# Two output weights placed above the normed rows, the rows in pieces, and key chunks of 272, 256 and 512 columns

## The chip, the cores and the metric

The kernel runs on one core of one Trainium2 chip. The metric is the device time of one execution in microseconds (us), the median of the runs shown. The core's engines work side by side, each through a queue of its own in a fixed order: TensorE (PE in the profile; PEld is its loading of weights), VectorE (DVE), ScalarE (ACT), GpSimd (POOL), and SyncE (SP), which here only issues transfers. Matmuls write to PSUM banks of 128 x 512 float32; everything else that is worked on lies in SBUF.

## The reference

One layer of a hybrid encoder over 1024 rows of width 1024, with 16 learned rows in front (1040 in all):

```
u     = rms_norm(h, norm_mix_w)
proj  = u @ w_in                       # fq fk fv ff hq hf hi hg
fox   = attention(fq, fk, fv, log_sigmoid(ff + bias))   # 8 heads x 64, causal,
                                       # score + sum of log f between key and query
hgrn  = rms_norm(recurrence(hq, hf, hi)) * silu(hg)     # 4 heads, 128 x 128 state
h     = h + concat(fox, hgrn) @ w_out
u     = rms_norm(h, norm_ffn_w)
h     = h + (silu(u @ w_gate) * (u @ w_up)) @ w_down    # 2816 wide
out   = rms_norm(h, norm_final_w)[16:]
```

All inputs and outputs are float32.

## The kernel before, in words

Every product of float32 matrices is made of three matmuls: each operand is split into a rounded part (hi) and the rest (lo), and `mm3` (L171 to L173) adds hi·hi, hi·lo and lo·hi. The split of an operand is one cast on ACT and one subtraction on DVE (`split`, L139 and L140).

The stages, in the order in which they are written:

1. Rows are normed, transposed by PE and kept as `u`, two tiles (hi and lo) of 8 x 1136 columns each, in a pool of their own (`uT`). For odd row tiles a mirrored copy is made on POOL (L256).
2. The recurrence, head by head (`hgrn_proj`, `hgrn_compute`), and the values of the attention (`fox_v`).
3. The attention in four pairs of heads. `fox_proj` multiplies `u` by a pair's key and query weights (`form1`): the keys in the chunks of `FULL`, the queries in the two chunks of `REAL`. The first chunk of each is made at once; the rest (`rest()`: two key chunks, one of queries) is written after group 0 of the pair. Keys and queries of pairs 0 and 2 lie in the pool `fxk0`, those of 1 and 3 in `fxk1`. `fox_compute` runs four groups of 256 query rows, each for both heads: scores (L577, L578), the gate bias with a running minimum on DVE (L583), the exponential on ACT (L588), transposes (L596, L608), a split (L612, L613), and the product with the values (L618). Group g needs keys up to 16 + 256(g + 1).
4. The output projection. Its eight weight blocks (128 rows of `w_out` each) go through a staging tile `w_st` (two of them in the pool `w1`, used by every weight of the kernel), then a cast (L691) and two subtractions (L693) by `load_wo`. Blocks 4 to 7 belong to the recurrent heads, 0 to 3 to the attention. `out_half` multiplies the recurrent half of row tiles 0 and 1 and keeps the sums in `halves`; `out_proj` does the rest, tile by tile in `ORDER`, and adds the residual.
5. Norm, then the gated feed-forward in Strassen-like block products, whose sums and splits are made on DVE and ACT (`pair`, `ffn_sums`, `ffn_load`), the down projection, and the last norm.

SBUF is shared between pools that are opened and closed like stacks, one from the left and one from the right. A tile of a new pool waits for the last readers of the tiles that lay in its place. So the pools `op` (working tiles of the output stage) and `wo` (its weights), which take the place of `uT`, can be written only after `rest()` of the last pair has read `u` for the last time. They are opened by `after_group`, which `fox_compute` calls behind each group of the last pair:

```
def after_group(g):
    if g == 0:
        uT_pool.__exit__(None, None, None)
        op, wo = op_pool.__enter__(), wo_pool.__enter__()
        load_wo(WO1)          # blocks 4, 5, 6, 7
    if g == 1:
        out_half(ORDER[:2])
        load_wo(WO2)          # blocks 0, 1, 2, 3
```

The order on each engine, and that of the transfers on SP, is set when the program is built. What is written earlier goes first, unless by the planner's own estimate it isn't ready and something later is; so dense products written after a group are put between its steps, where their operands are planned to be there. On the chip the order stays, even where the times come out otherwise.

Of the kernel before, what the change touches and what calls it, by code (L numbers as in the profile page):

```python
# [25 lines left out]
UW = U0 + L  # L26
NT = SEQ // P
# [12 lines left out]
WO1 = (4, 5, 6, 7)  # L40
WO2 = (0, 1, 2, 3)
# [6 lines left out]
def f32(ap):  # L48
    return ap.bitcast(F32)
# [3 lines left out]
def hybrid_trunk(  # L53
# [64 lines left out]
    uT_pool = left("uT")  # L118
    uT = uT_pool.__enter__()
    u = (uT.tile([P, KT, UW], F32R, name="u_hi"), uT.tile([P, KT, UW], F32R, name="u_lo"))  # L120

# [20 lines left out]
    def norm_transpose(u, xt, rows, wb, xn_pool, col):  # L142
# [6 lines left out]
        for g in range(2):  # L149
            pt = bank("tr")  # L150
            p3 = pt.rearrange("p (k t) -> p k t", t=P)
            for k in range(4):
                pe.transpose(p3[:, k, :rows], xn[:rows, (4 * g + k) * P:(4 * g + k + 1) * P], ident[:rows, :rows])
            hi = u[0][:, 4 * g:4 * g + 4, col:col + rows]
            act.copy(hi, p3[:, :, :rows])
            vec.tensor_sub(u[1][:, 4 * g:4 * g + 4, col:col + rows], p3[:, :, :rows], f32(hi))
# [18 lines left out]
    def form1(u, w, c0, n):  # L175
        o = dense()
        hi, lo = w
        for k in range(KT):
            mm3(o[:, :n], hi[:, k, :], lo[:, k, :], u[0][:, k, U0 + c0:U0 + c0 + n], u[1][:, k, U0 + c0:U0 + c0 + n], k == 0, k == KT - 1)
        return o[:, :n]  # L180

    FULL = ((0, 272), (272, 384), (656, 384))
# [13 lines left out]
    def form2(w, col, c0, n, rows=P, v=u):  # L196
        o = dense()
        for k in range(KT):
            mm3(o[:rows, :n], v[0][:, k, col:col + rows], v[1][:, k, col:col + rows],
# [3 lines left out]
    def meta_stack(um):  # L203
        pool.memset(f32(um), 0.0)
        for r0, s_ in zip((0, 32), u):
# [13 lines left out]
    with ExitStack() as norm_ctx:  # L219
# [4 lines left out]
        def hi_tile(slot, rows, col):  # L224
# [3 lines left out]
            else:  # L228
                v, col = (flips.pop(slot), 0) if slot in flips else (u, col)
                act.copy(hvt, form2(whi, col, 0, 512, rows, v))  # L230
# [9 lines left out]
        for i, (slot, rows, col) in enumerate(TILES):  # L240
# [9 lines left out]
            norm_transpose(u, xt, rows, wb, npool, col)  # L250
# [101 lines left out]
    def hgrn_proj(h):  # L352
# [4 lines left out]
        for c0, n in FULL:  # L357
            o = form1(u, w, c0, n)
# [12 lines left out]
        for (c, sc, tag, lst) in ((C_HQ, float(P) ** -0.5, "hg_q", qs), (C_HG, 1.0, "hg_s", sgs)):  # L371
            w = load_m(c + h * P, w_in[0])
            for c0, n in REAL:
                o = form1(u, w, c0, n)
# [139 lines left out]
    def fox_proj(p, fxk):  # L514
# [7 lines left out]
        def keys(i):  # L522
            c0, n = FULL[i]
            o = form1(u, wk, c0, n)
# [4 lines left out]
        def queries(i):  # L529
            c0, n = REAL[i]  # L530
            o = form1(u, wq, c0, n)
# [151 lines left out]
    wos, op, wo = {}, None, None  # L683

    def load_wo(ks):
        for k in ks:
            st = w1.tile([P, D], F32, name="w_st", tag="w_st")
            sync.dma_start(out=st, in_=w_out[0, k * P:(k + 1) * P, :])
            hi = wo.tile([P, D], F32R, name=f"woh{k}")
            lo = wo.tile([P, D], F32R, name=f"wol{k}")  # L690
            act.copy(hi, st)  # L691
            for hs in (slice(0, 512), slice(512, 1024)):
                vec.tensor_sub(lo[:, hs], st[:, hs], f32(hi[:, hs]))  # L693
            wos[k] = (hi, lo)

    halves = {}
    op_pool, wo_pool = left("op", 2), left("wo")

    def out_half(ts):
        mt, mh, ml = (op.tile([P, KT, P], d, name=n_, tag=n_, bufs=1) for n_, d in (("mt", F32), ("mh", F32R), ("ml", F32R)))  # L700
# [4 lines left out]
        for i, t in enumerate(ts):  # L705
            halves[t] = op.tile([P, D], F32, name="h2", tag="h2")
            for hs in (slice(0, 512), slice(512, 1024)):
                o = dense()
                for k in range(4):
                    j = 4 * i + k  # L710
                    mm3(o, mh[:, j, :], ml[:, j, :], wos[4 + k][0][:, hs], wos[4 + k][1][:, hs], k == 0, k == 3)
                act.copy(halves[t][:, hs], o)

    def after_group(g):
        nonlocal op, wo
# [25 lines left out]
    wb2 = op.tile([P, D], F32, name="wb2", bufs=1)  # L741
    sync.dma_start(out=wb2, in_=norm_ffn_w[0, :].partition_broadcast(P))

    def out_proj(t):
        ts_ = slice(t * P, (t + 1) * P)
        mt = op.tile([P, KT, P], F32, name="mt", tag="mt", bufs=1)
        mh = op.tile([P, KT, P], F32R, name="mh", tag="mh", bufs=1)
        ml = op.tile([P, KT, P], F32R, name="ml", tag="ml", bufs=1)
# [4 lines left out]
        ht = op.tile([P, D], F32, name="ht", tag="ht")  # L753
# [19 lines left out]
    def norm2_first(t, ht=None, keep_psum=False):  # L773
        if ht is None:
            ht = op.tile([P, D], F32, name="h2", tag="h2")
            sync.dma_start(out=ht, in_=h_dram[t])
        s = op.tile([P, KT, P], F32, name="sT", tag="ml" if t == 7 else "sT", bufs=1)
# [7 lines left out]
        xn = op.tile([P, D], F32, name="xn", tag="h2")  # L785
# [39 lines left out]
    def ffn_raw(m):  # L825
        sts = []
        for wsrc in (w_ffn_gate, w_ffn_up):
            st = w1.tile([P, KT, P], F32, name="w_st", tag="w_st")
# [50 lines left out]
    for i, t in enumerate(ORDER):  # L879
        if i < NT - 1:  # L880
            hts[ORDER[i + 1]] = out_proj(ORDER[i + 1])
        else:
            wo_pool.__exit__(None, None, None)
# [5 lines left out]
        p_, tag = ((w1, "w_hi"), (w1, "w_lo"), (op, "mt"), (op, "mh"))[t - 4]  # L889
        tas[t - 4] = p_.tile([P, KT, P], F32, name=f"ta{t}", tag=tag, **({"bufs": 1} if p_ is op else {}))  # L890
        if t < 6:
            s_, pts_, = norm2_rest(norm2_first(t, hts[t], True))
# [8 lines left out]
    spare = [op.tile([P, KT, P], F32R, name=n_, tag=n_) for n_ in ("h2", "ht")]  # L901
    raw1 = ffn_raw(1)
# [19 lines left out]
    op_pool.__exit__(None, None, None)  # L922
# [281 lines left out]
```

## Time and profile before

| | us |
|---|---|
| runs | 1296.81, 1296.89, 1297.60 |
| median | 1296.89 |
| the profiled execution | 1297.19 |
| its span, first to last instruction | 1295.2 |
| PE busy | 1263.7 (98%) |
| DVE busy | 908.6 (70%) |
| ACT busy | 620.8 (48%) |

The profile is of one execution. Its lines name the line of the kernel, the engine, the operation, the tiles (written <- read) and the shape. In the lists of waits the columns are: the engine and tile that waited, what it waited for, us in total, times, longest. In the windows they are: the stretch and its length, then busy us and instructions of PE, PEld, DVE, ACT and POOL, the mean clock granted to TensorE (1.00 is full), the busy share of the transfer engines, and GB/s. A list of a single tile's instructions leaves out the engines that have none. In timelines: start, duration, engine, line, operation, and in brackets the idle time before it with what ended it. The last pair of heads lies at about 496 to 582 us, the output stage from there to about 651, and the feed-forward begins there.

### The profile page before, as it was taken

The numbers are of one execution on the slowest core, as the hardware profiler recorded it, in microseconds if no ns is written. First come the engines' busy times: TensorE is split into PE (matmuls) and PEld (weight loads), VectorE is DVE, ScalarE is ACT, GpSimd is POOL, SyncE is SP. The second block draws the span as 40 slices with busy tenths as digits, with TensorE's granted clock in tenths as the row PEclk, the third lists the DMA queues.
The fourth block names the chain that finished last, engine by engine and source line by source line (L and its number), as shares of the span: only waits on it lengthen the run. The fifth ranks groups of instructions, "written<-read, shape, count | busy, mean of one in ns | idle before, by whom it ended". The sixth has DMA issues, their size and how long they took to land.

```text
span 1295.2 us, 18497 instructions
## 1 busy us (share of the span) xinstructions
PE 1263.7 (98%) x6553; PEld 1066.5 (82%) x6553; DVE 908.6 (70%) x1889; ACT 620.8 (48%) x1334; POOL 126.4 (10%) x260
## 2 busy tenths in 40 slices
PE   8999999999899999899999999999999999999997
PEld 6888898988788888778868888888888888888886
DVE  6467666575597877796788766666666664697777
ACT  6356656464567666664453333233323333443364
POOL 1220101010334342210000000000000000000000
PEclk8999999999999999999999999999999999999999
DMA  7231212123222121533314323333332337854452
GB/s 255 74 115 45 73 42 74 58 60 115 66 92 63 59 63 47 180 111 116 127 49 139 123 82 121 122 111 106 118 122 74 114 122 265 305 194 147 122 170 82
DMA packets 135196, 146.37 MB, mean 113 GB/s; under 512 B 6984, under 2 KB 95368, under 8 KB 135104
## 3 DMA queue, kind: packets, MB, share of 16 engines
q1 hardware_dynamic: 135104, 145.19, 34.4%
q8 instruction: 52, 0.85, 0.3%
q14 instruction: 40, 0.33, 0.1%
HBM read 105.98 MB, written 39.19 MB: 112 GB/s over the span
## 4 chain that ended last, share of the span: by engine, by line
PE 81%; DVE 9%; ACT 4%; issue 2%; DMA 2%; POOL 1%; SPq 0%; DVEq 0%; ACTq 0%; POOLq 0%
PE pb L171 10%; PE pb L173 10%; PE pb L172 10%; PE dense L173 8%; PE dense L171 8%; PE dense L172 8%; PE g L171 4%; PE g L172 4%; PE g L173 4%; PE o L618 3%; PE tr L608 2%; PE g L577 1%; PE g L578 1%; DMA w_st<-in_w_in_dram 1%; PE o L172 1%
## 5 line engine op out<-in xcount | busy, mean ns | idle before, releaser
L172 PE MATMUL dense<-u_lo,w_hi 128*128 128x512 f32 (+2 forms) x384 | 141.0, 367 | 0.0
L171 PE MATMUL dense<-u_hi,w_hi 128*128 128x512 f32 (+2 forms) x384 | 140.2, 365 | 0.0
L173 PE MATMUL dense<-u_hi,w_lo 128*128 128x512 f32 (+2 forms) x384 | 139.5, 363 | 0.0
L172 PE MATMUL pb<-T_lo,bh 128*128 128x512 f32 x352 | 137.3, 390 | 0.3 <-DVE T_lo L140 0.2
L173 PE MATMUL pb<-T_hi,bl 128*128 128x512 f32 x352 | 136.9, 389 | 0.1
L171 PE MATMUL pb<-T_hi,bh 128*128 128x512 f32 x352 | 136.8, 390 | 0.2 <-ACT bh L139 0.2
L139 ACT CAST bh<-sS 128x512 fp32r<-128x512 f32 x88 | 54.3, 621 | 150.2 <-DVE sS L846 69.3
L139 ACT CAST h_hi<-h_st 128x1024 fp32r<-128x1024 f32 (+1 forms) x43 | 41.8, 972 | 82.3 <-PE o L172 37.8
L172 PEld LDWEIGHTS pb<-T_lo,bh 128*128 128x128 f32 x352 | 66.1, 188 | 15.0 <-DVE T_lo L140 1.2
L171 PEld LDWEIGHTS pb<-T_hi,bh 128*128 128x128 f32 x352 | 66.0, 188 | 14.4 <-ACT bh L139 0.6
L173 PEld LDWEIGHTS dense<-u_hi,w_lo 128*128 128x128 f32 x384 | 72.5, 189 | 6.2
L173 PEld LDWEIGHTS pb<-T_hi,bl 128*128 128x128 f32 x352 | 66.1, 188 | 14.0 <-DVE bl L140 0.4
L172 PEld LDWEIGHTS dense<-u_lo,w_hi 128*128 128x128 f32 x384 | 72.8, 190 | 5.8
L171 PEld LDWEIGHTS dense<-u_hi,w_hi 128*128 128x128 f32 x384 | 72.8, 190 | 5.7
L171 PE MATMUL pb<-w_hi,h_hi 128*128 128x512 f32 x198 | 77.0, 389 | 0.0
L172 PE MATMUL pb<-w_lo,h_hi 128*128 128x512 f32 x198 | 77.0, 389 | 0.0
L173 PE MATMUL pb<-w_hi,h_lo 128*128 128x512 f32 x198 | 77.0, 389 | 0.0
L140 DVE TENSOR_TENSOR w_lo<-w_st,w_hi 128x1024 fp32r<-128x1024 f32 (+1 forms) x41 | 49.8, 1214 | 36.8 <-ACT w_hi L139 36.6
L140 DVE TENSOR_TENSOR h_lo<-h_st,h_hi 128x1024 fp32r<-128x1024 f32 (+1 forms) x43 | 48.3, 1123 | 29.2 <-ACT h_hi L139 28.6
L139 ACT CAST w_hi<-w_st 128x1024 fp32r<-128x1024 f32 (+1 forms) x47 | 48.9, 1041 | 40.0 <-PE dense L172 17.3
L171 PE MATMUL g<-B_hi,w_hi 128*128 128x512 f32 x168 | 65.7, 391 | 0.8 <-ACT p L874 0.7
L172 PE MATMUL g<-B_lo,w_hi 128*128 128x512 f32 x168 | 65.4, 389 | 0.0
(861 smaller groups left out, 3344.1 us busy)
## 6 DMA issues: line engine op xcount, KB each, us to landing
w_st<-in_w_in_dram SPq DMA_DIRECT2D x24, 512.0 KB, 4.0
w_st<-in_w_ffn_gate_dram SPq DMA_DIRECT2D x22, 512.0 KB, 3.7
w_st<-in_w_ffn_up_dram SPq DMA_DIRECT2D x22, 512.0 KB, 3.9
B<-in_w_ffn_down_dram SPq DMA_DIRECT2D x20, 512.0 KB, 6.1
h_st<-S SPq DMA_DIRECT2D x20, 512.0 KB, 3.8
h_st<-A SPq DMA_DIRECT2D x15, 512.0 KB, 4.3
A<-g SPq DMA_DIRECT2D x22, 256.0 KB, 2.0
S<-u SPq DMA_DIRECT2D x22, 256.0 KB, 2.9
```

The source lines that it names most:

```text
L139: later(act.copy(hi, src))
L140: return later((engine or vec).tensor_sub(lo, src, f32(hi)))
L171: pe.matmul(o, lhsT=ah, rhs=bh, start=first, stop=False, skip_group_check=skip)
L172: pe.matmul(o, lhsT=ah, rhs=bl, start=False, stop=False, skip_group_check=skip)
L173: pe.matmul(o, lhsT=al, rhs=bh, start=False, stop=last, skip_group_check=skip)
L577: pe.matmul(sc[:, :w], lhsT=QA[:, P * i:P * (i + 1)], rhs=KS[:, c0:c0 + w], start=True, stop=False)
L578: pe.matmul(sc[:, :w], lhsT=QB[:, P * ii:P * (ii + 1)], rhs=KS[:, c0:c0 + w], start=False, stop=True)
L608: pe.transpose(pt[:, o + ii * P:o + (ii + 1) * P], Ss[ii][:, c:c + P], ident)
L618: m = pe.matmul(ob[:, q0:256], lhsT=vt[:, blk, :], rhs=r[:, q0:256], start=blk == NT, stop=blk == 2 * g + 1 and i == 3)
```

## The change

- **Rows in pieces.** The pool of `u` becomes two, `uh` and `ul`, and the tiles six: `ua_hi` and `ua_lo` hold the first 640 columns (all 8 blocks of the depth), `ub_hi0`, `ub_hi1` (four blocks each) and `ub_lo` the other 496. `u_k` and `u_half` find the place. The writes of `norm_transpose` and the mirrored copies go by halves of the depth, so an odd row tile has four mirrored copies of half the size for two.
- **Key chunks.** `FULL` goes from 272, 384, 384 to 272, 256, 512, so that a chunk ends where the first piece ends.
- **Early part.** A new pool `woe` is opened above the two pools of `u`, in the place of `fxk0`, before the last pair. Into it go, ahead of `fox_compute(3)`, the recurrent half of row tiles 0 and 1 with its split (`half_parts`, taken out of `out_half`), and weight blocks 4 and 5.
- **The output stage takes the pieces' places.** After group 0, five wide tiles are opened, each over one piece; `Slots` hands out rows of 1024 numbers of them under the old names. Blocks 6 and 7 and the hi of block 0 lie over `ua_lo`; the lo of block 0, block 1 and the hi of block 2 over `ub_lo`; the lo of block 2 and block 3 over the three tiles of `half_parts`. Blocks 6 and 7 are loaded after group 0, blocks 0 to 3 after group 1, as before.
- **Start of the feed-forward.** The second gate weight is fetched into `mt` and not into `w_st`, its split goes to `mh` and `ml`, the working tiles of row tiles 6 and 7 to `h2` and `wb2`, and the scratch of row tile 7 to `ht`.

The core of the diff:

```diff
+UA = P + SEQ // 2
-WO1 = (4, 5, 6, 7)
-WO2 = (0, 1, 2, 3)
...
-    u = (uT.tile([P, KT, UW], F32R, name="u_hi"), uT.tile([P, KT, UW], F32R, name="u_lo"))
+    u_pools = left("uh"), left("ul")
+    uh, ul = (p_.__enter__() for p_ in u_pools)
+    ua_hi = uh.tile([P, KT, UA], F32R, name="ua_hi", tag="ua_hi")
+    ub_hi = [uh.tile([P, KT // 2, UW - UA], F32R, name=f"ub_hi{g}", tag=f"ub_hi{g}") for g in range(2)]
+    ua_lo = ul.tile([P, KT, UA], F32R, name="ua_lo", tag="ua_lo")
+    ub_lo = ul.tile([P, KT, UW - UA], F32R, name="ub_lo", tag="ub_lo")
+
+    def u_k(k, col, n):
+        if col < UA:
+            return ua_hi[:, k, col:col + n], ua_lo[:, k, col:col + n]
+        c = slice(col - UA, col - UA + n)
+        return ub_hi[k // 4][:, k % 4, c], ub_lo[:, k, c]
...
-    FULL = ((0, 272), (272, 384), (656, 384))
+    FULL = ((0, 272), (272, 256), (528, 512))
...
-                for f, s_ in zip(flips[slot], u):
-                    pool.tensor_copy(f[:, :, ::-1], s_[:, :, col:col + P])
+                for g in range(2):
+                    for f, s_ in zip(flips[slot], u_half(g, col, P)):
+                        pool.tensor_copy(f[:, 4 * g:4 * g + 4, ::-1], s_)
...
+    woe_pool = left("woe")
+    woe = woe_pool.__enter__()
+    wides = {}
+
+    class Slots:
+        def __init__(self, **tags):
+            self.tags = {tag: list(places) for tag, places in tags.items()}
+
+        def tile(self, shape, dtype, name, tag):
+            places = self.tags[tag]
+            places.append(places.pop(0))
+            wide, i = places[-1]
+            t = wides[wide][:, i, :]
+            return t if len(shape) == 2 else t.rearrange("p (k c) -> p k c", c=shape[2])
+
+    op = Slots(ht=[("ua_hi", 0), ("ua_hi", 1)], h2=[("ua_hi", 2), ("ua_hi", 3)], sT=[("ua_hi", 4)],
+               mt=[("ub_hi0", 0)], wb2=[("ub_hi0", 1)], mh=[("ub_hi1", 0)], ml=[("ub_hi1", 1)])
+    wo = Slots(wo=[("ua_lo", i) for i in range(5)] + [("ub_lo", i) for i in range(4)])
+
+    def open_wide():
+        for p_, n, dtype, tag in ((uh, 5, F32, "ua_hi"), (uh, 2, F32, "ub_hi0"), (uh, 2, F32R, "ub_hi1"),
+                                  (ul, 5, F32R, "ua_lo"), (ul, 4, F32R, "ub_lo")):
+            wides[tag] = p_.tile([P, n, D], dtype, name=f"wide_{tag}", tag=tag)
+
+    def load_wo(k, homes):
+        st = w1.tile([P, D], F32, name="w_st", tag="w_st")
+        sync.dma_start(out=st, in_=w_out[0, k * P:(k + 1) * P, :])
...
+    def half_parts(ts):
+        mt, mh, ml = (woe.tile([P, KT, P], d, name=f"half_{i}", tag=f"e{i}") for i, d in enumerate((F32, F32R, F32R)))
         for i, t in enumerate(ts):
             a = slice(4 * i, 4 * i + 4)
             sync.dma_start(out=mt[:, a, :], in_=mix_dram[4:8, :, t * P:(t + 1) * P].rearrange("k p c -> p k c"))
             split(mh[:, a, :], ml[:, a, :], mt[:, a, :])
...
     def after_group(g):
         if g == 0:
-            uT_pool.__exit__(None, None, None)
-            op, wo = op_pool.__enter__(), wo_pool.__enter__()
-            load_wo(WO1)
+            open_wide()
+            for k in (6, 7):
+                load_wo(k, (None, None))
         if g == 1:
             out_half(ORDER[:2])
-            load_wo(WO2)
-
+            for k, homes in enumerate(((None, None), (None, None), (None, "e0"), ("e1", "e2"))):
+                load_wo(k, homes)
+
+    half_parts(ORDER[:2])
+    for k in (4, 5):
+        load_wo(k, (f"woh{k}", f"wol{k}"))
     fox_compute(3, *b, None, None, after_group)
...
-        s = op.tile([P, KT, P], F32, name="sT", tag="ml" if t == 7 else "sT", bufs=1)
+        s = op.tile([P, KT, P], F32, "sT", "ht" if t == 7 else "sT")
...
-    spare = [op.tile([P, KT, P], F32R, name=n_, tag=n_) for n_ in ("h2", "ht")]
-    raw1 = ffn_raw(1)
+    tas[2:] = (op.tile([P, KT, P], F32, "ta", tag) for tag in ("h2", "wb2"))
+    spare = [op.tile([P, KT, P], F32R, n_, n_) for n_ in ("mh", "ml")]
+    raw1 = ffn_raw(1, op.tile([P, KT, P], F32, "mt", "mt"))
```

More of the change, by code (lines that the diff above doesn't have):

```diff
@@ L682, in hybrid_trunk @@
     fxk0_pool.__exit__(None, None, None)
[L683 to L694, printed above, removed]
@@ L888, in hybrid_trunk @@
             continue
[L889 to L890 removed]
         if t < 6:
+            tas[t - 4] = w1.tile([P, KT, P], F32, name=f"ta{t}", tag=("w_hi", "w_lo")[t - 4])
             s_, pts_, = norm2_rest(norm2_first(t, hts[t], True))
```

83 lines of the change are left out of this document (45 added, 38 removed).

## The prediction

> **What bounds the kernel now.** I read the page first, then the clock, the waits of TensorE (PE), windows over the stages, and last the timeline of each engine where PE was idle.
>
> ```profile
> span 1295.2 us, 18497 instructions
> PE 1263.7 (98%) x6553; PEld 1066.5 (82%) x6553; DVE 908.6 (70%) x1889; ACT 620.8 (48%) x1334; POOL 126.4 (10%) x260
> ```
>
> PE is busy 1263.7 of 1295.2 us. The change takes no matmul away, so it can win only from the 31.5 us in which PE idles, or from time at a lowered clock. The windows (PE, PEld, DVE, ACT, POOL busy, then PEclk, DMA share, GB/s) say where these are around the last pair of heads and after it:
>
> ```profile
> 489.00:500.00 11.00, 10.88 (x75) 9.76 (x74) 9.50 (x34) 7.98 (x15) 3.96 (x11) 1.00 0.04 13
> 500.00:514.00 14.00, 13.80 (x99) 12.31 (x98) 10.08 (x31) 8.08 (x22) 3.24 (x11) 1.00 0.30 88
> 514.00:520.50 6.50, 6.50 (x32) 5.57 (x32) 1.95 (x4) 1.31 (x3) 0.00 (x0) 1.00 0.07 23
> 520.00:525.00 5.00, 2.16 (x12) 1.43 (x10) 3.80 (x9) 4.21 (x8) 2.15 (x3) 1.00 0.64 165
> 525.00:530.00 5.00, 4.88 (x17) 4.06 (x17) 3.82 (x14) 0.60 (x2) 1.24 (x4) 0.66 0.97 330
> 530.00:535.00 5.00, 3.93 (x23) 3.06 (x23) 3.58 (x11) 4.42 (x9) 1.26 (x4) 1.00 0.70 197
> 535.00:580.00 45.00, 44.15 (x266) 35.96 (x265) 41.13 (x117) 31.12 (x66) 9.35 (x17) 1.00 0.37 118
> 580.00:651.40 71.40, 71.03 (x337) 58.02 (x336) 46.55 (x106) 31.39 (x78) 0.00 (x0) 1.00 0.36 120
> 651.40:683.00 31.60, 29.16 (x127) 21.78 (x126) 31.10 (x57) 19.66 (x38) 0.00 (x0) 1.00 0.21 67
> ```
>
> There are two holes: 2.84 us (5.00 - 2.16) at 520 to 525, followed by five microseconds at a mean clock of 0.66, and 1.07 us at 530 to 535. Around them PE is nearly full. A third, 2.44 us at 651 to 683, stands where VectorE (DVE) is full, 31.10 of 31.60. The waits of PE and the timelines of PE, ScalarE (ACT) and SyncE (SPq) name the first two:
>
> ```profile
> PE g L577 <- DVE mx L583: 1.5, 1, 1.5
> PE tr L596 <- ACT S__6390 L588: 1.3, 1, 1.3
> PE dense L171 <- ACT woh L691: 1.1, 1, 1.1
> PE g L171 <- ACT p L874: 1.4, 2, 0.7
> ...
> 520.32 0.39 PE L173 MATMUL dense<-u_hi,w_lo 128*128 128x512 f32 x1
> 525.14 0.71 PE L171 MATMUL dense<-woh,mh 128*128 128x512 f32 x1
> ...
> 521.24 1.98 ACT L691 CAST woh<-w_st 128x1024 fp32r<-128x1024 f32 x2
> 524.48 1.12 ACT L139 CAST mh<-mt 128x512 fp32r<-128x512 f32 x2
> 530.56 1.04 ACT L691 CAST woh<-w_st 128x1024 fp32r<-128x1024 f32 x1 [4.95 <-DMA w_st<-in_w_out_dram]
> 531.51 0.73 ACT L588 ACTIVATE S__6402<-S__6402,mx 128x528 f32<-128x528 f32 x1
> ...
> 462.70 5.75 SPq L688 DMA_DIRECT2D w_st<-in_w_out_dram  x2
> 520.74 0.93 SPq L703 DMA_DIRECT2D mt<-mix_dram  x2
> ```
>
> The last projection matmul that reads the normed rows starts at 520.32. Until then their pool can't be given up, so two output weights lie raw in both staging tiles from 462.70 on and are cast only at 521.24, the recurrent half is loaded at 520.74, and a third weight is fetched only when the first is cast. Group 1 of the last pair therefore has no dense matmul beside it: PE waits for its chain (1.5 and 1.3 us), and the first product of the output stage comes at 525.14. The cast at 530.56 then waits for its transfer, with the exponential of group 1 (531.51) queued behind it on ACT.
>
> **Loading early (half_parts, weights 4 and 5).** It adds nothing. Moved from 520-530 to the end of pair 2 are two 256 KB transfers and two 512 KB ones (these two are early already), four casts on ACT (1.98 + 1.12 = 3.1 us) and six subtractions on DVE:
>
> ```profile
> 522.58 2.18 DVE L693 TENSOR_TENSOR wol<-w_st,woh 128x512 fp32r<-128x512 f32 x3
> ```
>
> Three in 2.18 us are 0.7 each, so six are 4.2 us. Their places are the keys and queries of pair 2, free when its last scores are done at about 495; the first group of the last pair then runs to about 514. ACT has 3.0 + 5.9 us free in the first two windows above and DVE 1.5 + 3.9, so 3.1 and 4.2 us fit, tightly on DVE. PE is covered there by 72 projection matmuls, and from 514 to 520.5 it runs those alone: the attention may come 6.5 us later before the projections run out. I cost this at nothing; without that cover it is 4.2 us of DVE, all of it on PE's path.
>
> **Rows in pieces.** The first piece ends with the second key chunk. Its last reader is the middle key projection, whose eviction in the trace of before is done long before 520:
>
> ```profile
> 510.23 0.56 DVE L527 TENSOR_TENSOR KS<-dense,KS 64x384 fp32r<-64x384 f32 x1
> ```
>
> The second subtraction of the middle chunk starts at 510.23, so its matmuls end near 509, and with 256 columns for 384 earlier. Weights 6 and 7 take places of that piece. Their transfers need the staging tiles that 4 and 5 now give back near 500, so they land by about 508, and two casts and four subtractions (2.0 on ACT, 2.8 on DVE) fall at 510-520, where the two engines are 1.31 and 1.95 us busy of 6.50 from 514 on. By 520.5 all that out_half reads is ready. It is written after group 1, so it fills where group 1 waits: 48 matmuls, 10.9 us at 0.227 each, against holes of 2.84 and 1.07.
>
> What is won: the 2.84 us; the 1.07 us, whose transfer is no longer late; and the lowered clock:
>
> ```profile
> 526.00:527.00 1.00, 1.00 (x4) 0.73 (x3) 0.97 (x4) 0.00 (x0) 0.00 (x0) 0.50 0.88 287
> ```
>
> Five microseconds at a mean of 0.66 (525 to 530, above) lose 5 x 0.34 = 1.7 us; I take 1.6, since 0.12 of them are idle and counted already. The half clock follows four microseconds in which PE was idle for most. "TensorE: Matmul & The Clock Gate" of the Trainium skill (section "What's actually happening") says that the clock is halved after an idle window of about 3.4 us that runs freely, so whether these gaps trip it would be partly luck. By that rule alone the 1.6 might be no loss of every run, and the time would be 1293.2; the three runs lie within 0.8 us, which speaks for a loss that every run has.
>
> Does the work come back later? Only if the filler now used early is missed in groups 2 and 3. Of dense matmuls, the stretch of the last pair used
>
> ```profile
> 520.60:580.00 59.40, 30.92 (x101) 18.30 (x100) 4.01 (x6) 3.40 (x6) 0.97 0.47 147
> 580.00:651.50 71.50, 67.27 (x284) 52.42 (x284) 7.49 (x11) 0.00 (x0) 1.00 0.36 119
> ```
>
> 101, with 284 left after it. Those that need nothing of groups 2 and 3 are 48 (out_half) + 48 (the rest of tiles 0 and 1) + 24 (tile 4's recurrent half) = 120. Were the attention to end at 580 as now, PE would want 5.5/0.227 = 24 more, 125 in all: five short, 1.1 us. But DVE, 41.13 of 45.00 busy at 535-580, sheds 7.0 us (4.2 and 2.8) from 520 on, so the attention ends earlier too. I cost it at 0, ends 0 and +1.1.
>
> Weight 3 now lies where half_parts lay, so its cast waits for out_half's last product; it is the last of tile 0's four, 18 matmuls (4.1 us) behind the first, against 1.04 + 1.4 us of cast and subtractions. Nothing.
>
> **Key chunks.** From PE's timeline, starts of the first matmul of each run of 24, and 18 of 256 columns from another stage:
>
> ```profile
> 70.07 0.29 PE L171 MATMUL dense<-u_hi,w_hi 128*128 128x272 f32 x1
> 73.03 0.33 PE L171 MATMUL dense<-u_hi,w_hi 128*128 128x384 f32 x1
> 77.22 0.33 PE L171 MATMUL dense<-u_hi,w_hi 128*128 128x384 f32 x1
> 163.81 0.28 PE L171 MATMUL dense<-wvh,u_hi 128*128 128x256 f32 x1
> 165.95 0.28 PE L171 MATMUL dense<-wvh,u_hi 128*128 128x256 f32 x1
> ```
>
> 272 columns take 0.123 us, 384 take 4.19/24 = 0.175, 256 take 2.14/18 = 0.119, and 512 0.227. Per set of 24 that is 24 x (0.119 + 0.227 - 2 x 0.175) = -0.1 us; 8 sets, four of the recurrence and four of the attention: -0.8, or, with 0.173 as the later 384s run, -0.0. I take -0.2. Element counts of the evictions are unchanged.
>
> **The other places.** Two rows of the feed-forward's start:
>
> ```profile
> 654.73 0.38 SPq L829 DMA_DIRECT2D w_st<-in_w_ffn_gate_dram  x1
> 667.42 0.69 DVE L140 TENSOR_TENSOR T_lo<-ta,T_hi 128x512 fp32r<-128x512 f32 x1
> ```
>
> The mirrored copies on POOL become four of half size for two, and no wait for them is among PE's longer ones: 0, and as an estimate 0.3 either way. The second gate is fetched at 654.73 now; in the output stage's tile, free once the last row block is split, it comes several us sooner. PE's two waits there (1.4 in all, above) may go, but the product after them needs the split that DVE ends at 667.42 + 0.69 = 668.1, and DVE is full. So PE would wait there instead: 0, bounds -1.4 and, if the idle time gathers into one hole like that at 521, +1.6.
>
> **Sum.** -2.84 - 1.07 - 1.6 - 0.2 = -5.7; I keep 0.4 for a first wait that no filler reaches, so -5.3. The profiled execution took 1297.19 us (1295.2 and 2.0 around it), giving 1291.9; it lies 0.3 above the median of the runs, so 1291.6 is forecast.
>
> **The rivals.** *Part of it.* First two rows of GpSimd's copies of queries (for the group: minimum, median and maximum in ns):
>
> ```profile
> 523.48 0.73 POOL L563 CAST QB<-QA 64x256 fp32r<-64x256 f32 x1
> L563 POOL CAST QB<-QA x32: 392/394/734, 351.0 to 555.2; 64x256 fp32r<-64x256 f32 x32
> ```
>
> The two weights above arrive in time but 6 and 7 do not: group 1 meets filler only for its first hole, the clock stays, and the 1.07 or the feed-forward hole remains: -2.8 - 0.2, or 1293.9. For it: casts wait on ACT behind exponentials, as at 530.56 the other way round. "SBUF — State Buffer" of the Trainium skill ("Who interferes with whom") says that a VectorE operation with two SBUF inputs contends with GpSimd's reads, which speaks against moving subtractions beside group 0's copies of queries: at 523.48, beside three of them, such a copy took 0.73 against a median of 0.39, which agrees. By it six moved subtractions cost GpSimd up to 2 us and the time would be 1293.6 at worst; GpSimd is under half busy.
>
> *Given back.* DVE sets the end of the attention, the work moved early delays group 0 by what it saves later, and PE's idle time moves into groups 2 and 3: -0.2 to -1, or 1296.3. Against it stand the 6.5 us of spare cover from 514 to 520.5.
>
> *Slower: the load of the values stands behind a weight on SP.* SP's queue is served in order, and its transfers for weights waited long before:
>
> ```profile
> SPq L688 <- DVE wol L693: 14.4, 6, 5.0
> 508.19 0.38 SPq L544 DMA_DIRECT2D v<-v_dram  x1
> 513.10 0.36 PE L618 MATMUL o<-mz,v 128*128 128x256 f32 x1
> ```
>
> The values of the last pair's second head are asked for at 508.19, the moment their place is free, and PE multiplies with them at 513.10, in a fixed order. Weights 6 and 7, or the halves, now stand near them in the queue; one that waits for a staging tile delays the values, and each us late idles PE for one. From 5.3 us (about one wait of 5.0 and its issue) the gain is gone; two such waits, 10 us, and the halved clock after them (1.6) give +6.3, or 1303.
>
> **Chances.** Forecast (1289 to 1293) 0.56, part 0.16, given back 0.14, slower 0.14. Measurement tells 0.2%, 2.6 us, from no change: faster 0.70 (the forecast and nearly all of "part", which stands at that bound), same 0.16, slower 0.14. Forecast with the bounds of the unpriced terms (-1.4, -0.6, -0.3) reaches down to 1288.9; upward the range takes in part and most of given back: 1288.8 to 1297.5.
>
> **What would show it.** In the changed profile PE is full from 520 to 535 at clock 1.00, first products from woh start within about 1 us of the last projection, casts of weights 4 and 5 lie before 514 and those of 6 and 7 before 521; the wait of PE for woh is gone; DVE's busy time from 535 on falls. Idle time of PE at 555-580, a dip of its clock anywhere past 20 us, or a wait for v at group 0 would show the rivals.

## The result, and the profile after

The median went from 1296.81 to 1288.95 us (five runs each); the ratio on record is 0.9945, with a 95% interval of 0.9934 to 0.9955. The forecast was 1291.6, in a range of 1288.8 to 1297.5. The profiled execution of the changed kernel took 1289.45 us, its span 1287.7.

The first view is the windows of the changed kernel (PE, PEld, DVE, ACT, POOL busy, then PEclk, DMA share, GB/s), with two of the kernel before behind the dots; the second is PE's and ACT's timeline of the changed kernel around the end of the projections.

```profile
340.00:350.00 10.00, 7.77 (x35) 6.31 (x34) 5.45 (x9) 5.03 (x13) 3.13 (x2) 0.88 0.27 79
520.00:530.00 10.00, 10.00 (x52) 7.80 (x50) 7.64 (x27) 7.51 (x16) 3.15 (x8) 1.00 0.49 141
530.00:540.00 10.00, 9.54 (x57) 7.84 (x57) 8.45 (x19) 5.60 (x13) 2.48 (x4) 1.00 0.71 208
550.00:560.00 10.00, 10.00 (x70) 8.81 (x68) 9.53 (x32) 7.82 (x21) 2.55 (x6) 1.00 0.20 73
560.00:570.00 10.00, 9.77 (x63) 7.99 (x62) 9.55 (x33) 7.78 (x16) 1.04 (x2) 1.00 0.08 22
650.00:660.00 10.00, 8.32 (x41) 6.57 (x39) 9.96 (x20) 7.99 (x15) 0.00 (x0) 1.00 0.35 101
660.00:670.00 10.00, 9.79 (x35) 7.38 (x34) 10.00 (x18) 3.71 (x8) 0.00 (x0) 0.83 0.01 2
...
340.00:350.00 10.00, 9.65 (x60) 8.19 (x58) 3.41 (x11) 4.88 (x18) 3.29 (x2) 1.00 0.47 131
660.00:670.00 10.00, 8.97 (x38) 6.17 (x37) 10.00 (x17) 8.92 (x18) 0.00 (x0) 1.00 0.00 0
```

```profile
522.92 0.39 PE L188 MATMUL dense<-ub_hi,w_lo 128*128 128x512 f32 x1
523.74 0.40 PE L186 MATMUL dense<-woh,half 128*128 128x512 f32 x1
...
498.85 1.05 ACT L728 CAST woh<-w_st 128x1024 fp32r<-128x1024 f32 x1
504.74 1.05 ACT L728 CAST woh<-w_st 128x1024 fp32r<-128x1024 f32 x1
506.42 1.05 ACT L728 CAST wide_ua_lo<-w_st 128x1024 fp32r<-128x1024 f32 x1
512.12 1.04 ACT L728 CAST wide_ua_lo<-w_st 128x1024 fp32r<-128x1024 f32 x1
```

The hole at 520 to 535 is gone: PE is full from 520 to 530 at full clock (and busy 9.54 of the next 10.00), the last projection starts at 522.92 and the first product of the output stage 0.8 us behind it, with all four weights cast by 513.2. But two new places show a lowered clock, 340 to 350 (0.88) and 660 to 670 (0.83), and 340 to 350 has a hole of 2.2 us that the kernel before doesn't have there.

To see where the time went I took PE's timeline matmul by matmul. The usual distance from one start to the next is 0.227 us at 512 columns, 0.175 at 384, 0.124 at 272, 0.118 at 256 and 0.057 for a transpose; what lies beyond it is lost. The streaming itself is 1166.3 us before and 1165.4 after. The lost time, in us, is cut by the streaming that is still to come, so that the rows compare the same work. The chunks and the feed-forward's places alone are on the kernel before, the other three on the changed kernel:

| stage (about, us, in the kernel before) | before | after | chunks alone | 6 and 7 in late places | rows in late places | feed-forward's places alone | pair 1 on VectorE |
|---|---|---|---|---|---|---|---|
| up to pair 2 (0-461) | 84.65 | 87.67 | 87.84 | 88.54 | 87.44 | 84.02 | 84.71 |
| pair 2 (461-516) | 10.09 | 10.40 | 10.26 | 10.17 | 10.54 | 10.06 | 10.40 |
| end of the projections (516-545) | 8.45 | 2.82 | 7.71 | 2.59 | 3.63 | 7.72 | 2.51 |
| rest of the last pair (545-587) | 7.92 | 6.20 | 7.70 | 6.79 | 6.05 | 8.78 | 6.25 |
| output stage (587-651) | 3.54 | 2.15 | 4.00 | 2.30 | 2.15 | 3.43 | 2.15 |
| feed-forward's start (651-687) | 5.80 | 5.30 | 5.80 | 5.07 | 4.26 | 7.30 | 4.26 |

The experiments that the last five columns belong to follow below. So the change won 5.6 where it was aimed, then 1.7 and 1.4 behind it, 0.5 at the feed-forward's start and 0.9 of streaming, and it lost 3.0 before 461 and 0.3 in pair 2. With 0.4 in the rest that is 7.2 of the 7.5 us between the two spans. Neither the chunks nor the feed-forward's places take the hole at 520 away by themselves (7.71 and 7.72 lost there) or win behind it (11.70 and 12.21 from 545 to 651, 11.46 before, 8.35 after). By elimination it is the rest of the change that does both: the rows in pieces with the early loads and their places, taken together; whether it needs the chunks or those places beside it wasn't tried.

### The profile page after: what moved, and what is told of

Read it like the earlier page. It is cut to its first block, busy times and chain, and to the rows that moved or that the text cites. A ratio compares the mean times of both kernels' runs of the same rounds, so it can differ in the third digit from the quotient of the medians.

```text
span 1287.7 us, 18543 instructions
## 1 busy us (share of the span) xinstructions
PE 1260.4 (98%) x6553; PEld 1061.7 (82%) x6553; DVE 909.0 (71%) x1889; ACT 620.8 (48%) x1334; POOL 128.1 (10%) x268
## 4 chain that ended last, share of the span: by engine, by line
PE 85%; DVE 6%; ACT 5%; issue 1%; DMA 1%; POOL 1%; SPq 0%; DVEq 0%; ACTq 0%; POOLq 0%
PE pb L188 11%; PE pb L186 11%; PE pb L187 11%; PE dense L186 9%; PE dense L187 9%; PE dense L188 9%; PE g L186 4%; PE g L187 4%; PE g L188 4%; PE o L633 2%; PE tr L623 2%; PE g L592 1%; PE g L593 1%; PE tr L168 1%; PE o L188 1%
## 5 line engine op out<-in xcount | busy, mean ns | idle before, releaser
L186 PE MATMUL dense<-ua_hi,w_hi 128*128 128x512 f32 (+2 forms) x224 | 77.5, 346 | 0.0
L187 PE MATMUL dense<-ua_lo,w_hi 128*128 128x512 f32 (+2 forms) x224 | 76.8, 343 | 0.0
L188 PE MATMUL dense<-ua_hi,w_lo 128*128 128x512 f32 (+2 forms) x224 | 76.2, 340 | 0.0
L188 PE MATMUL g<-B_hi,w_lo 128*128 128x512 f32 x168 | 65.4, 389 | 0.0
L188 PE MATMUL dense<-ub_hi,w_lo 128*128 128x512 f32 x160 | 64.4, 403 | 0.0
L187 PE MATMUL dense<-ub_lo,w_hi 128*128 128x512 f32 x160 | 64.3, 402 | 0.0
```

Of the source, the lines that this page charges most:

```text
L186: pe.matmul(o, lhsT=ah, rhs=bh, start=first, stop=False, skip_group_check=skip)
L187: pe.matmul(o, lhsT=ah, rhs=bl, start=False, stop=False, skip_group_check=skip)
L188: pe.matmul(o, lhsT=al, rhs=bh, start=False, stop=last, skip_group_check=skip)
```

## The experiments

**The chunks alone**, on the kernel before:

```diff
-    FULL = ((0, 272), (272, 384), (656, 384))
+    FULL = ((0, 272), (272, 256), (528, 512))
```

> The kernel before with one line changed, the key chunks 272, 256, 512 for 272, 384, 384. Theory (the gain of the last pair comes from its loads, the chunks are worth next to nothing): 0 to -0.8 us against the kernel before, in the window 525 to 529 the clock is still halved and the hole of PE at 520 to 525 is still there. Rival (the chunks carry what the prediction did not find, some 2 us): -2 us or more, spread evenly over the eight sets, so that the first store of the last recurrent head lies 1 us earlier already.

1298.15 us against 1296.46, ratio 1.0016 (1.0007 to 1.0025). Both were wrong: this part costs time. The loss of 3.2 us up to 461, in the table, is nearly that of the changed kernel (3.0), and in both one new hole stands out. First DVE, POOL and PE of the changed kernel, then DVE and POOL of the kernel before:

```profile
341.80 2.35 DVE L110 TENSOR_TENSOR rs_t<-rs_y 128x4 f32<-128x4 f32 x1 [0.47 <-ACT rs_y L109]
...
341.75 2.38 POOL L155 TENSOR_TENSOR w_lo<-w_st,w_hi 128x1024 fp32r<-128x1024 f32 x1 [29.97 <-ACT w_hi L154]
...
345.92 0.59 PE L524 MATMUL tr<-ident,hE 128*128 128x128 f32 x2 [2.23 <-ACT hE L521]
```

```profile
342.94 0.16 DVE L111 TENSOR_TENSOR rs_t<-rs_y 128x4 f32<-128x4 f32 x1 [0.51 <-ACT rs_y L110]
...
338.80 2.37 POOL L140 TENSOR_TENSOR w_lo<-w_st,w_hi 128x1024 fp32r<-128x1024 f32 x1 [26.53 <-ACT w_hi L139]
```

The norm at the end of the last recurrent head squares four numbers per partition. That took 0.16 us before and 2.35 after, because GpSimd subtracts the low part of a weight of the next pair at that moment (the weights of pairs 1 to 3 are split with GpSimd in VectorE's place): the two end together, at 344.15 and 344.13. The chunks had moved this subtraction from 338.80 to 341.75 and the norm's product from 342.94 to 341.80, so that the one now starts 0.05 us ahead of the other. Then PE has a hole of 2.23 us, since the norm's scaled rows are what it waits for.

**Taking the collision away.** The low parts of pair 1's two weights are subtracted on VectorE; first on the chunks alone, then on the changed kernel, then on the kernel before:

```diff
-        wk, wq = (load_m(c + p * P, w_in[0], pool if p else None) for c in (C_FK, C_FQ))
+        wk, wq = (load_m(c + p * P, w_in[0], pool if p > 1 else None) for c in (C_FK, C_FQ))
```

> The kernel before with the key chunks 272, 256, 512 and, beside that, the low parts of pair 1's key and query weights subtracted on VectorE instead of GpSimd. Theory (the chunks alone cost time because they move one such subtraction of 2.38 us on GpSimd beside the last norm of the recurrence, where a 128x4 product on VectorE then lasts 2.35 us instead of 0.16, PE stands for 2.4 us and its clock is halved for the 3.413 us behind it): the product takes 0.16 us again, the hole at 343.7 shrinks to under 1 us, no halved clock near 347, and 2 to 3.5 us less than with the chunks alone, so 0 to -1.5 us against the kernel before. Rival (the longer 512-column evictions, or the order of the matmuls, make the hole): the hole stays over 1.5 us and the time within 0.7 us of the chunks alone.

> The changed kernel with the same subtractions on VectorE. Theory: the hole at 343.7 and the halved clock behind it go, 2 to 3.5 us less than the changed kernel, near 1286. Rival (as above): within 0.7 us of the changed kernel.

> The kernel before with the low parts of pair 1's key and query weights subtracted on VectorE. It completes the square of chunks and this edit. Theory (in the kernel before the subtraction on GpSimd lay at 338.8, beside work of VectorE that reads PSUM, and held nothing up): within 1 us of the kernel before, so that the chunks are worth about -2 us where the collision is out of the way. Rival (GpSimd's subtraction costs about 2 us in every kernel, and the chunks are worth nothing): -1.5 to -3 us.

They took 1294.52 us (ratio to before 0.9984, 0.9975 to 0.9992), 1284.26 (0.9904, 0.9889 to 0.9919) and 1297.04 (1.0003, 0.9994 to 1.0011). The changed kernel with this one line, DVE, PE and windows:

```profile
342.97 1.23 DVE L155 TENSOR_TENSOR w_lo<-w_st,w_hi 128x1024 fp32r<-128x1024 f32 x1 [0.36 <-ACT w_hi L154]
344.12 0.15 DVE L110 TENSOR_TENSOR rs_t<-rs_y 128x4 f32<-128x4 f32 x1
...
346.05 0.33 PE L524 MATMUL tr<-ident,hE 128*128 128x128 f32 x1 [0.20 <-ACT hE L521]
...
340.00:350.00 10.00, 9.80 (x58) 8.36 (x57) 6.03 (x12) 5.99 (x20) 0.00 (x0) 1.00 0.26 79
```

The product takes 0.15 us again, PE waits 0.20 instead of 2.23, the clock stays at 1.00, and 3.0 of the lost microseconds up to 461 are back. The collision is shown: the edit changes only where these subtractions run, and it wins 3.6 us on the chunks and 4.7 on the changed kernel, more than the 2 to 3.5 expected, but nothing on the kernel before, where the two didn't meet. In lost time up to 461 the edit wins 4.7 us on the chunks and 0.7 on the kernel before, so the collision costs about 4. The 3.0 of the table are less because they are a balance: over the work that lies at 336 to 352 in the kernel before, PE loses 5.3 us there, 6.4 in the changed kernel and 2.7 with the line, since the kernel before has another wait in this stretch. Between the two profiled executions of the changed kernel, whose spans differ by 4.3 us, another 1.0 lies at the feed-forward's start (4.26 for 5.30), where the clock stayed full this time; that is not the edit's, as told below. With the collision away the chunks are worth about 2.5 us by the medians (1294.52 against 1297.04), 0.9 of it streaming. The rest isn't settled: the spans of the two profiled executions are the same (1293.5), the runs of the kernel before with the edit spread from 1294.8 to 1299.0, and the edit also takes away that other wait of the kernel before, for a copy of queries that stands behind the second weight on GpSimd:

```profile
351.89 0.51 PE L578 MATMUL g<-KS,QB 128*128 128x256 f32 x2 [1.98 <-POOL QB L564]
```

**Loading later**, on the changed kernel: all loads written behind group 0, or weights 6 and 7 behind group 1.

```diff
             open_wide()
+            half_parts(ORDER[:2])
+            for k in (4, 5):
+                load_wo(k, (f"woh{k}", f"wol{k}"))
...
-    half_parts(ORDER[:2])
-    for k in (4, 5):
-        load_wo(k, (f"woh{k}", f"wol{k}"))
```

```diff
-            for k in (6, 7):
-                load_wo(k, (None, None))
         if g == 1:
+            for k in (6, 7):
+                load_wo(k, (None, None))
```

> The changed kernel with the loads of the recurrent half and of weights 4 and 5 moved behind group 0 of the last pair, ahead of weights 6 and 7; all places as in the changed kernel. Theory (loading early and the places carry the gain of the last pair): four casts of weights and two of rows then queue after 514, the first product of the output stage comes 2 to 5 us after the last projection, PE is idle 1.5 to 3 us there, and 3 to 5 us of the 7.9 are gone. Rival (the place above the rows is enough, since weights may be fetched before the projections end): under 1 us is lost.

> The changed kernel with weights 6 and 7 loaded behind group 1 of the last pair, just ahead of the first products of the output stage, and not behind group 0; weights 4, 5 and the rows stay early. Theory (the loads only have to come before the projections end; the second gain, 1.9 us between 550 and 563, comes from casts and subtractions that are out of the way of groups 2 and 3): transfers and casts of two weights move some 6 to 8 us later, beside groups 1 and 2; the first products of the output stage still start on time with weights 4 and 5, then wait for weight 6 for 0 to 2 us, and about 1 us of the 1.9 comes back: +0.5 to +3 us against the changed kernel. Rival (the places alone do it): within 0.5 us of it.

1290.01 (ratio 0.9951, 0.9939 to 0.9964) and 1289.19 us (0.9942, 0.9930 to 0.9955): +1.1 and +0.2 against the changed kernel. Neither tested what it was meant to, because the planner put the work nearly where it had been. In the second the casts of 6 and 7 came at 506.34 and 512.03. In the first the casts of 4 and 5 came at 499.25 and 507.56 (498.85 and 504.74 in the changed kernel); only those of 6 and 7 moved, to 514.48 and 519.20, and still came before the last projection. Its 1.1 us lie at 505.79, not behind the projections (2.48 lost there):

```profile
505.79 0.39 PE L593 MATMUL g<-KS,QB 128*128 128x256 f32 x1 [1.34 <-POOL QB L579]
```

There PE waits 1.34 us for GpSimd's copy of queries. So where the loads are written matters little here; how early they have to be is not shown by these two.

**Places instead of order.** Weights 6 and 7 get places that the last projection reads, or the recurrent rows do:

```diff
-    wo = Slots(wo=[("ua_lo", i) for i in range(5)] + [("ub_lo", i) for i in range(4)])
+    wo = Slots(wo=[("ub_lo", i) for i in range(4)] + [("ua_lo", i) for i in range(5)])
```

```diff
-        mt, mh, ml = (woe.tile([P, KT, P], d, name=f"half_{i}", tag=f"e{i}") for i, d in enumerate((F32, F32R, F32R)))
+        mt, mh, ml = (op.tile([P, KT, P], d, n_, n_) for n_, d in (("mt", F32), ("mh", F32R), ("ml", F32R)))
...
             open_wide()
+            half_parts(ORDER[:2])
...
-    half_parts(ORDER[:2])
```

> The changed kernel with the two pieces' places for weights exchanged: weights 6 and 7 take those of the second piece of the low parts, which is read until the last projection, and weights 0 to 2 those of the first piece. The two runs with loads written later left the casts of weights 6 and 7 almost where they were (506.4 and 512.1, or 514.5 and 519.2), so they didn't test what the place is worth. Theory (the places above the rows carry the gain, since the casts can come before the projections end): the casts of 6 and 7 come behind the last projection, near 523, the first products of the output stage wait for weight 6, a hole of PE of 1 to 3 us at 521 to 527, perhaps a halved clock of 1.7 behind it, and +1.5 to +5 us against the changed kernel. Rival (weights 4 and 5 with their rows are enough, the rest of the gain is relief of VectorE): under +0.7 us.

> The changed kernel with the recurrent rows of the first two row tiles in the output stage's own working tiles, which lie in the second pieces of the high parts and are read until the last projection; all weights stay as in the changed kernel. So the first products of the output stage can only start some 3 us behind the last projection (a transfer of 2 us and a cast of 1.05). Theory (the hole of PE at 520 to 527 goes because rows and two weights are ready before the projections end, whichever of the others come later): the hole is back, PE loses 3 to 6 us more between 521 and 535, a halved clock among them in most runs, +2.5 to +6 us against the changed kernel. Rival (relief of VectorE and the earlier weights carry the gain): under +1 us.

1289.94 us (ratio 0.9950, 0.9937 to 0.9964) and 1290.42 (0.9955, 0.9942 to 0.9969), +1.0 and +1.5, between theory and rival in both, and within the intervals of the ratios. From 516 to 651 the two profiles lose only 0.5 and 0.7 us more than the changed kernel's; the rest of the difference lies elsewhere or between runs. ACT of the first, then PE of the second:

```profile
523.60 1.05 ACT L728 CAST wide_ub_lo<-w_st 128x1024 fp32r<-128x1024 f32 x1 [4.23 <-PE dense L187]
525.16 1.04 ACT L728 CAST wide_ub_lo<-w_st 128x1024 fp32r<-128x1024 f32 x1
```

```profile
524.49 0.39 PE L592 MATMUL g<-KS,QA 128*128 128x272 f32 x1 [0.84 <-DVE mx L598]
525.29 0.40 PE L186 MATMUL dense<-woh,wide_ub_hi 128*128 128x512 f32 x1
```

The delays are there, as expected: two casts behind the last projection, or first products 2.6 us behind it (522.66 to 525.29). The hole isn't: 2.59 and 3.63 us lost, against 8.45 before. So neither of these two loads alone carries the gain. With weights 6 and 7 late, the products with 4 and 5 reach until they are cast; with the rows late, only their two casts, 1.13 us in all, are added on ACT behind the last projection, where the kernel before had five (1.98, 1.12 and 1.04 us), the last of them for a weight fetched late. The hole of before took rows and weights together; how few of them bring it back wasn't tried.

**The feed-forward's start**: its places alone, on the kernel before, and the changed kernel with the second gate in a staging tile.

```diff
...
-        p_, tag = ((w1, "w_hi"), (w1, "w_lo"), (op, "mt"), (op, "mh"))[t - 4]
-        tas[t - 4] = p_.tile([P, KT, P], F32, name=f"ta{t}", tag=tag, **({"bufs": 1} if p_ is op else {}))
         if t < 6:
+            tas[t - 4] = w1.tile([P, KT, P], F32, name=f"ta{t}", tag=("w_hi", "w_lo")[t - 4])
...
-    spare = [op.tile([P, KT, P], F32R, name=n_, tag=n_) for n_ in ("h2", "ht")]
-    raw1 = ffn_raw(1)
+    tas[2:] = (op.tile([P, KT, P], F32, name="ta", tag=tag, **kw) for tag, kw in (("h2", {}), ("wb2", {"bufs": 1})))
+    spare = [op.tile([P, KT, P], F32R, name=n_, tag=n_, bufs=1) for n_ in ("mh", "ml")]
+    raw1 = ffn_raw(1, op.tile([P, KT, P], F32, name="mt", tag="mt", bufs=1))
```

```diff
-    raw1 = ffn_raw(1, op.tile([P, KT, P], F32, "mt", "mt"))
+    raw1 = ffn_raw(1)
```

> The kernel before with only the places of the feed-forward's start changed: the second gate is fetched into the output stage's tile, its parts take the two row tiles, the sums of the last two tiles take the places of the norm. Theory of the prediction: 0 (between -1.4 and +1.6), PE waits for the product with T2 instead of the gate. Rival (the output stage and the feed-forward's start won about 1.7 us of the 7.9 by themselves): -1.2 to -2 us, with PE idle 1 to 1.5 us less between 650 and 680.

> The changed kernel with the second gate of the feed-forward fetched into a staging tile, as before the change; all else as changed. Theory (the early fetch of the gate pays for itself only if PE would wait for it): PE waits about 0.7 us twice near 650 to 658 for the cast of the gate, +0.5 to +1.5 us against the changed kernel; the hole of 1.7 us before the product with T2 gets smaller by as much, and with it the halved clock after it may go, so that 0 or even -1 is possible. Rival (the gate's fetch is what the feed-forward's start gained): +1.5 to +2.5 us.

1297.83 us (ratio 1.0011, 1.0002 to 1.0019) and 1289.71 (0.9950, 0.9936 to 0.9963). Waits of PE, in this order: the changed kernel, the gate in a staging tile, the places on the kernel before.

```profile
659.55 0.73 PE L186 MATMUL pb<-T_hi,bh 128*128 128x512 f32 x2 [1.68 <-ACT T_hi L154]
```

```profile
650.18 0.50 PE L186 MATMUL g<-B_hi,w_hi 128*128 128x512 f32 x1 [0.68 <-ACT p L913]
657.81 0.50 PE L186 MATMUL g<-B_hi,wide_ub_hi 128*128 128x512 f32 x1 [0.68 <-ACT p L913]
```

```profile
666.58 1.35 PE L171 MATMUL pb<-T_hi,bh 128*128 128x512 f32 x2 [3.02 <-ACT T_hi L139]
660.00:670.00 10.00, 6.98 (x28) 5.13 (x27) 10.00 (x18) 7.32 (x13) 0.00 (x0) 0.81 0.00 0
```

The early gate takes two waits of 0.68 away and gathers them, and more, into one for the product with T2, while DVE is full (10.00 of 10.00). In lost time this stretch is 5.02 us with the gate in a staging tile; with the early gate it is 4.22 to 4.26 in five profiles whose clock stays full here, and 5.02 to 5.30 in the three where it is halved behind the hole. So the early gate is worth the 0.8 us between the medians, or nothing; the intervals of the two ratios overlap. On the kernel before that hole is 3.02 us, the clock is halved behind it, and the places cost 1.4.

**Reordering that start**: the split for B22 and the two subtractions for T4 of the last two tiles are written behind what T2, T3 and the first sums need; then the same together with pair 1's weights on VectorE.

```diff
-        put("B22", t, b22)
-        sub(t2, t2, b21[0])
-        sub(t2, t2, b21[1])
-        return done
+        def rest():
+            put("B22", t, b22)
+            sub(t2, t2, b21[0])
+            sub(t2, t2, b21[1])
+        if t < 2:
+            rest()
+        return done, rest
...
     ffn_splits(sums[0], range(4))
+    rest2()
+    rest3()
```

> The changed kernel with seven operations of the last two row tiles (the split for B22 and the two subtractions for T4, for each of the two) written behind what T2, T3 and the first sums need. Theory (from 650 to 666 VectorE is the bound, every operation there is 0.6 us on the path to the product with T2): that product starts 1.5 to 2.5 us earlier, the hole of 1.7 us at 658 to 659.5 goes and with it the halved clock at 661.6 to 665, together 1.5 to 3.5 us less than the changed kernel. Rival (the product then meets the operations that were put off, in T3 or T4): within 0.7 us of the changed kernel.

> The changed kernel with pair 1's weights on VectorE and the feed-forward's start reordered. Theory (the reordering wins only where the clock would have been halved behind the hole at 658): 1283.3 to 1284.5, 0 to -1 us against the kernel with the weights on VectorE alone, no halved clock between 20 and 1270. Rival (both gains add up in full): under 1283.

1288.73 us (0.9940, 0.9928 to 0.9953), 0.2 below the changed kernel, and 1284.76 (0.9911, 0.9898 to 0.9925), against 1284.26 with the one line alone. The first wait shrank only from 1.68 to 1.48, and one of 0.64 came at 666.78. The rival was right: what was put off is met again, DVE is busy all the time (10.00 of 10.00 in the windows of 660 to 670 above), and its order hardly matters. The fastest version of the study is the changed kernel with pair 1's weights on VectorE; with the reordering it is the same within the noise.

## Why the prediction was right or wrong

**The end of the projections, -5.5 and 0.4 kept.** In size right: -5.6. What was to show it did: PE full from 520 to 530, first product 0.8 us behind the last projection, the wait for woh gone, the clock there at 1.00. A dip of the clock past 20 us, named as a sign of the rivals, came too (347.55 and 661.57), but for reasons that no rival held. Two steps of the working fell.

- The 1.6 us for the halved clock are no term of their own. The chunks alone with pair 1's weights on VectorE, and the feed-forward's places alone, have no halved clock in this stretch and lose 8.3 and 7.7 us there; the kernel before and the chunks alone have it and lose 8.5 and 7.7. My reading is that a slower PE costs little while it waits for ACT and DVE in any case. The loss that I split in three is one.
- "By 520.5 all that out_half reads is ready" was taken to be needed. It isn't: weights 6 and 7 cast at 523.6 and 525.2 cost 0.5 us in the stages behind and 1.0 between the medians. The rival *Part of it*, whose price was the same lateness, would have come to some +1 and not the 2.3 us between its time and the forecast.

**The filler, 0 to +1.1.** Wrong in sign: the rest of the last pair lost 1.7 us less, and the output stage 1.4. The kernel before has a wait of 0.6 us at 560, for DVE, and two of 0.19 in the output stage; the changed kernel has one of 0.28, at 570. The argument had the right side: DVE did shed work. From just ahead of the last projection to the end of the attention, for the same matmuls, first the kernel before and then the changed one:

```profile
520.00:580.00 60.00, 55.11 (x313) 44.52 (x312) 52.34 (x148) 40.35 (x82) 14.00 (x25) 0.97 0.47 146
522.69:575.12 52.43, 51.66 (x313) 43.08 (x311) 46.35 (x140) 34.79 (x75) 13.08 (x25) 1.00 0.35 107
```

DVE is 6.0 us less busy (the step had 7.0) and ACT 5.6. What was wrong is the price: the filler was set at nothing or a loss, and less work on DVE beside the groups was worth a gain. That this relief is the cause is argued, not shown: with weights 6 and 7 late, whose subtractions then lie behind the last projection, the rest of the last pair lost 6.79 for 6.20, a part of the way back to 7.92. The output stage's share is 2.15 to 2.30 in every kernel with the rows in pieces and 3.4 to 4.4 in every other; which part of the change does it wasn't tried.

**The key chunks, -0.2.** This is the step that failed. By the rows the prediction had 0 to -0.8 of streaming and chose -0.2; by the usual distances it came to -0.9. But the 512-column chunk moved a subtraction on GpSimd by 3 us, onto VectorE's norm. That cost about 4 us, 3.0 after what else changed up to 461: about +2 in all, the +1.7 of the chunks alone. "Element counts of the evictions are unchanged" asked how much work there is and not when it runs and beside what. The prediction did weigh this very rule, of "SBUF — State Buffer" in the Trainium skill (section "Who interferes with whom"), but only for the last pair's copies of queries. The Trainium skill says more there than was used: the shared port is an exclusive lock, and the order of issue decides who waits. The trace agrees: GpSimd at 341.75, VectorE at 341.80, held until GpSimd is done.

**The feed-forward's start, 0 with -1.4 to +1.6.** Right, mechanism and bounds. With the change -0.5, on the kernel before alone +1.4 to +1.5: there the idle time did gather into one hole with a halved clock behind it, as the upper bound had it.

**Copies on POOL, 0.** Nothing is lost up to 312 us (51.0 us in both).

**The rivals.** The weights did stand in front of the loads of the values on SP, which were issued at 503.00 and 509.90 instead of 501.21 and 508.19, but PE didn't wait for them: its two waits from 496 to 524 are 0.23 us for DVE and 0.26 that the profile puts down to nothing. *Given back* did not happen. So the forecast came out 2.6 us high, with errors against each other: about 2.3 us too good at the chunks, 3.1 too bad behind the hole, and some 0.5 too bad at the hole and at the feed-forward each; the rest is small, in stages that had no term. The lower end itself holds a gap: 1291.6 less 1.4, 0.6 and 0.3 is 1289.3, and only with the 0.4 kept back taken off too does it come to the 1288.9 written. That the time lies in the range, 0.15 above its lower end, is luck: with the collision taken away by one line the changed kernel takes 1284.26, 4.5 below the range, which is 12.8 and not 5.3 better than the kernel before with the same line (1297.04).

## What to carry to other kernels

A change of tile sizes also moves every operation of the side engines in time: before pricing it by its own streaming, list the long GpSimd operations near it and the VectorE operations with two SBUF operands on the path beside them. Where VectorE is nearly full, look behind the hole too: here the stages after it gave 3.1 us beside its 5.6. And the hole at the feed-forward's start, where DVE's schedule is full, was moved, split or gathered by places and order, but not removed.

## What the runs showed of the hardware

**The halved clock goes by a fixed grid.** Ten of the fourteen profiles have halved stretches between 30 and 1270 us. All of them last 3.413 us, or twice that, and lie on a grid of 3.413 us that runs through the whole execution: in the changed kernel from 16.454 to 347.546 are 97.0 steps. Windows of the changed kernel on its grid:

```profile
344.13:347.55 3.42, 1.63 (x9) 1.34 (x10) 1.52 (x6) 1.14 (x4) 0.00 (x1) 1.00 0.58 151
347.55:350.96 3.41, 3.41 (x15) 3.23 (x14) 1.13 (x2) 2.08 (x3) 1.71 (x1) 0.50 0.21 79
658.16:661.57 3.41, 1.81 (x5) 0.93 (x6) 3.41 (x7) 3.40 (x8) 0.00 (x0) 1.00 0.00 0
661.57:664.99 3.42, 3.42 (x9) 2.65 (x9) 3.42 (x7) 2.14 (x5) 0.00 (x0) 0.50 0.02 5
```

A window decides on the next one. Worked out from the matmuls' columns, PE streamed for 1.18 and 1.13 us in the first and third. Between 30 and 1270 us, all fourteen windows of these profiles with 1.19 us of streaming or less were followed by a halved one; above that, from 1.21 us, only two were (1.29, and 1.39 in a window that was halved itself). So in these profiles the bound lies near a third of the window, and it isn't quite sharp. "TensorE: Matmul & The Clock Gate" in the Trainium skill (section "What's actually happening") says that the window is 3413 ns and runs freely, which agrees. The idle window of about 3.4 us that the Trainium skill names there wasn't needed here: a hole of 1.68 us, with slow products around it, was enough at 658. How the grid cuts a hole decides: holes of 2.2 to 2.3 us that end near 346 were followed by a halved clock in seven of the eight profiles that have one; in the eighth, of the reordered start, a step of the grid falls into the hole, at 345.02, and the windows on its two sides stream for 2.06 and 1.85 us. This may be one reason why runs of one kernel differ by 1 to 2 us; it wasn't tested.

**A long GpSimd operation can stretch a tiny one of VectorE fifteenfold**: 128x4 in 2.35 us beside GpSimd's 2.38, and 0.16 elsewhere. Where one operand of VectorE's came from PSUM, beside the same subtraction at 338.80, the kernel before shows no such stretch: a subtraction of 64x384 took 0.56 us at 339.57, and 0.55 at 337.80, ahead of it.
